# One layer of a gated linear attention trunk on one core: input rows in long runs, the first key half in the auxiliary banks, and same-place stretches of 12 products for 24

## Chip, cores and metric

One core of a Trainium2 chip (trn2). The metric is the device time of one execution in microseconds; lower is better. An execution of the kernel before takes 1075.46 us (median of three).

## What is computed

One layer on 256 tokens of width 2048: a gated linear attention mixer, then an MLP with a squared ReLU, then a final RMS norm. All weights and inputs are float32. Cut to what matters:

```python
h = rmsnorm(x, gla_norm)
proj = h @ w_in                      # q 1024, k 1024, v 2048, r 2048, g_low 16 columns
log_a = log_sigmoid(g_low @ w_gate_up + b_gate) / 16
# in chunks of 64 tokens, 4 heads:
k_dec = k * exp(total - cum)         # cum: running sum of log_a, total: its last value
state = exp(total) * state + k_dec.T @ v
o = q @ state
x = x + (rmsnorm(o, o_norm) * silu(r)) @ w_out
a = relu(rmsnorm(x, mlp_norm) @ w_up)          # 8192 columns
x = x + (a * a) @ w_down
return rmsnorm(x, final_norm)
```

## The kernel before

**Split products.** Every float32 operand of a large product is split into two parts, `hi` (rounded by ScalarE, line 109) and `lo` (the remainder, by VectorE, line 110). A product of two numbers becomes three on TensorE: `hi*hi`, `hi*lo`, `lo*hi`. Nearly all of TensorE's 9285 instructions are such products of a 128x128 stationary operand with 256 columns of a moving operand. "A product" below is one of them.

**Phases.** The work is a chain of phases on TensorE. In a *natural* phase (`natural`, products recorded on L140) tokens are stationary and a weight tile of 128 rows and 1024 columns moves: 16 steps, one for each 128 rows of the weights, and per step 2 token tiles x 3 products x 4 column quarters = 24 products. In a *turned* phase (`turned`, L169) the weights are stationary and the 256 tokens move: 8 weight tiles of two blocks of 128 rows and 512 columns, 24 products for each tile, 12 for each block. The order of phases:

1. first natural phase (half of the values and the gate's low-rank columns, 1040 columns wide), from the start to 53 us
2. turned: two halves of the keys (53 to 97 us), two halves of the queries (to 142 us)
3. natural: columns 3 x KEYW (other half of the values, to 193 us), 4 x KEYW and 5 x KEYW (the two halves of r, for the silu), then the two halves of `w_out`
4. the MLP in four rounds of 2048 hidden columns: four turned phases `up` (q 0 to 3), then `down` in two halves.

**Side work.** Small jobs (the gate's transposes and logits, `scores`, `attend`, the transposes of `turn`, the norm's `scale2_row`) wait in the queue `side`; `pump` issues one after each step (natural) or block (turned) of the main work. What is recorded is then put in order, engine by engine, by a scheduler with its own estimate of times; TensorE, ScalarE, VectorE and the DMA queue of SyncE each run their list in order.

**Where operands lie.** `OFF` is 48. Token tiles of the natural phases start 48 floats behind a multiple of 64 (`xth`, `xtl`: offset `OFF`, rows of `ROW` = 320 floats), and moving weight tiles start on a multiple of 64. In turned phases stationary weight tiles are written at `OFF` and moving tokens start on a multiple of 64. So the offset of the stationary operand, modulo 64 floats, is 48 and that of the moving one 0. Some steps break this: there both operands lie on the same offset. They are called *same-place* here:

```python
def row_x(kt):
    return [xe[:, i] for i in range(2)] if kt == EVEN else [a[:, kt, :T] for a in (xth, xtl)]
...
wh, wl = weights(w[...], 2 * GT, off=0 if kp in even else OFF)
```

`xe` holds a copy of token tile `EVEN` = 5 on a multiple of 64, for both token tiles of its step; in `turned` the argument `even` names weight tiles that are written without the offset. For `w_out` the same is done by `row_o`. In the 3 x KEYW phase step `EVEN` is put at place 11 (`late.insert(11, EVEN)`), elsewhere it stands at place 5. Each of these steps or tiles is a stretch of 24 same-place products.

**Banks.** Six PSUM banks (`acc_banks`) are given out in turn to the phases, two (`aux_bank`) to warm-up and side jobs. The first natural phase uses all six; its results leave by `put_v` (L306 on ScalarE, L307 on VectorE), and the first key half then takes the first two of the six. `turn_gate` (L334) and `gate_logits` (L343) use auxiliary banks.

**Start.** TensorE runs `WARM` products of a tile of ones (L195, two rows of the trace each). The input, transposed on the host, lies as 2048 rows of 256 floats, so a tile of 128 rows takes runs of 1 KB; tiles are loaded in groups (`x_loads`), tile 1 on ScalarE's DMA queue, the others on SyncE's between the weight tiles. The first weight tile comes in three pieces.

Of the kernel before, what the change touches and what calls it, by code (L numbers as in the profile page):

```python
# [27 lines left out]
F32 = mybir.dt.float32  # L28
F32R = mybir.dt.float32r
# [3 lines left out]
P = 128  # L33
T = 256
# [26 lines left out]
ROUNDS = HID // D  # L61
WARM = 9
FINE = 3
# [3 lines left out]
def tile_gla_mlp(ctx, tc, x, xt, cols, w_vg, w_in, w_gate, w_out, w_up, w_down, final_norm, out):  # L67
# [33 lines left out]

    def slots(off=0):
        return [wpool.tile([P, SLOT], F32R, tag=i, name=i)[:, off:] for i in ("hi", "lo")]

# [13 lines left out]

    def weights(src, n, pieces=None, room=None, skip=0, raw=None, off=0):

        to = room or slots(off)
        if raw is None:
            if not raw_half:
                raw_half.extend(raw_pair())
            raw = raw_half.pop(0)
        for s in (slice(*p) for p in pieces or [(0, n)]):
            dst = raw[:, s]
            if len(src.shape) == 3:
                dst = dst.rearrange("p (i c) -> p i c", i=2)
                last_load[0] = nc.sync.dma_start(out=dst, in_=src)  # L130
            else:
                last_load[0] = nc.sync.dma_start(out=dst, in_=src[:, s])  # L132
        return parts(raw, n, to, pieces or [(skip, n)])

    def halves(o, x, w, first, last):

        n = w.shape[-1]
        for c in range(0, n, T) if n % T == 0 else (0,):
            m = slice(c, c + T) if n % T == 0 else slice(0, n)
            nc.tensor.matmul(o[:, m], x, w[:, m], start=first and c == 0, stop=last, skip_group_check=True)  # L140

    def natural(row, source, n, cuts, pumps=1, ahead=None, order=range(KT)):

        acc = acc_banks(NT * len(cuts))
        acc = [acc[t * len(cuts) : (t + 1) * len(cuts)] for t in range(NT)]
        for step, kt in enumerate(order):
            wh, wl = weights(source(kt), n, ahead and ahead(kt))
            for t in range(NT):
                sh, sl = (a[:, t * P : (t + 1) * P] for a in row(kt))
                for i, (s, w) in enumerate(((sh, wh), (sh, wl), (sl, wh))):  # L150
                    for c, (lo, hi) in enumerate(cuts):
                        halves(acc[t][c], s, w[:, lo:hi], step == 0 and i == 0, step == KT - 1 and i == 2)
            if step < KT - 1:
                pump(pumps)
        return acc

    def turned(ah, al, w, c0, even=(0,)):

        acc = acc_banks(GT // P // 2)
        for kp in range(KT // 2):  # L160
            wh, wl = weights(w[2 * kp * P : 2 * (kp + 1) * P, c0 : c0 + GT].rearrange("(i p) c -> p i c", p=P), 2 * GT, off=0 if kp in even else OFF)
            for i in range(2):
                kt = 2 * kp + i
                for j in range(GT // P):
                    s = slice(i * GT + j * P, i * GT + (j + 1) * P)
                    o = acc[j // 2][:, j % 2 * T : (j % 2 + 1) * T]
                    for n, (u, m) in enumerate(((wh, ah), (wh, al), (wl, ah))):

                        nc.tensor.matmul(  # L169
                            o, u[:, s], m[:, kt], start=kt == 0 and n == 0 and j % 2 == 0,  # L170
                            stop=kt == KT - 1 and n == 2, skip_group_check=True,
                        )
                if kt < KT - 1:
                    pump()
        return acc
# [36 lines left out]

    xe = mid.tile([P, 2, T], F32R, tag="xe", name="xe")

    def row_x(kt):
        return [xe[:, i] for i in range(2)] if kt == EVEN else [a[:, kt, :T] for a in (xth, xtl)]

# [10 lines left out]

    xv = xt.rearrange("(kt p) t -> p kt t", p=P)
    xr = zz.rearrange("p a b t -> p (a b) t")  # L230
    cuts = [(0, 512), (512, 768), (768, WMAX)]
    x_done = [0]
    x_loads = {0: 1, 2: 4, 4: 6, 5: 8, 6: 12, 8: KT}
    nc.scalar.dma_start(out=xr[:, 1, :], in_=xv[:, 1, :])

    def input_tile(kt):
        if kt in x_loads:
            s = slice(x_done[0] if kt > 2 else kt, x_loads[kt])
            nc.sync.dma_start(out=xr[:, s, :], in_=xv[:, s, :])
            x_done[0] = x_loads[kt]  # L240
        if kt == KT - 1:
            wrap_input(0, KT - 2)
        nc.scalar.activation(xth[:, kt, :T], xr[:, kt, :], AF.Copy, scale=g1(kt))
        nc.vector.scalar_tensor_tensor(
            xtl[:, kt, :T], xr[:, kt, :], g1(kt), xth[:, kt, :T].bitcast(F32), op0=ALU.mult, op1=ALU.subtract
        )
        if kt == EVEN:
            nc.scalar.copy(xe[:, 0], xth[:, kt, :T].bitcast(F32))
            nc.vector.tensor_copy(xe[:, 1], xtl[:, kt, :T].bitcast(F32))
        return [(0, 256), (256, 512), (512, WMAX)] if kt == 0 else [(0, 512), (512, WMAX)] if kt < FINE else None  # L250

# [215 lines left out]

    late = [kt for kt in range(KT) if kt != EVEN]
    late.insert(11, EVEN)
    acc = natural(row_x, rows(w_in, 3 * KEYW), G, HALF, order=late)  # L470
    flush()
# [38 lines left out]
    def turn(src, row, gain, q):  # L510
# [5 lines left out]
        for i in range(2):  # L516
            kt = 2 * q + i
            s = b[:, i * T : (i + 1) * T]
# [12 lines left out]

    gain_o = lambda kt: go(kt % 4)
    side.extend([lambda: None] + [lambda q=q: turn(on, row_o, gain_o, q) for q in range(4)])
    acc = natural(row_x, rows(w_in, 5 * KEYW), G, HALF)
    flush()
    gate_out(acc, G)


    side.extend([lambda q=q: turn(on, row_o, gain_o, q) for q in range(4, 8)])
    hs = const.tile([P, NT, 4], F32, name="hs")  # L540

# [16 lines left out]
    hth, htl = (big.tile([P, KT, T], F32R, tag="A" + i, name="h" + i, bufs=1) for i in "hl")  # L558
    row_h = lambda kt: [a[:, kt, :] for a in (hth, htl)]
    side.extend([lambda: None] + [lambda q=q: turn(h, row_h, g2, q) for q in range(4)])  # L560
    side.append(lambda: ssq_h(0))
    acc = natural(row_o, rows(w_out, G), G, HALF)
    flush()
    add_h(acc, G)
    side.extend([lambda q=q: turn(h, row_h, g2, q) for q in range(4, 8)])
    r2 = const.tile([P, NT], F32, name="r2")
# [236 lines left out]
```

## Time and profile before

| | |
|---|---|
| time, median of 3 | 1075.46 us (1075.1 to 1075.59) |
| profiled execution, its own time | 1075.4 us |
| its span, first to last instruction | 1073.3 us |
| mean granted TensorE clock | 0.998 |
| TensorE busy | 1063.1 us, 99% |
| VectorE busy | 774.9 us, 72% |
| ScalarE busy | 573.7 us, 53% |
| data moved by DMA | 210.43 MB, mean 196 GB/s |

A line of a group reads: source line, engine, operation, output <- inputs, shape, count, then busy time and mean duration, then the idle time of the engine before it and what ended it. A line of the timeline reads: start, duration up to the last end, engine and operation, count. Products of TensorE overlap: each is under way for some 0.28 us while the next starts after some 0.11 to 0.12 us, so their durations do not add up; distances between starts do. A line of the windows gives the stretch, its length, the mean of PE, and busy time with a count for PE, PEld, DVE, ACT and POOL, then the granted clock, the DMA share and GB/s.

### The profile page before, as it was taken

How to read it: one execution, taken by the hardware profiler on the slowest of the kernel's cores; microseconds unless marked ns; L12 is line 12 of the kernel's file. 1: busy time of each engine (PE TensorE's matmuls, PEld its weight loads, DVE VectorE, ACT ScalarE, POOL GpSimd, SP SyncE). 2: the span in 40 equal slices, each digit the busy share in tenths (PEclk: the TensorE clock that was granted, in tenths of full speed). 3: DMA queues.
4: the chain of work that ended last, by engine and by line, in shares of the span. 5: the costliest groups of instructions: out<-in, count | busy, mean ns of one | idle time of the engine just before them, and what ended most of it. 6: DMA issues, size and time to landing. Idle time of an engine off the chain costs nothing.

```text
span 1073.3 us, 21863 instructions
## 1 busy us (share of the span) xinstructions
PE 1063.1 (99%) x9285; PEld 1062.3 (99%) x9285; DVE 774.9 (72%) x1027; ACT 573.7 (53%) x694; POOL 12.7 (1%) x39
## 2 busy tenths in 40 slices
PE   9999999999999999999999999999999999999997
PEld 9999999999999999999999999999999999999997
DVE  6668644556555466789986679986779997678874
ACT  6675444546444454556554456564555554555552
POOL 0000000000000000000000000000000000000000
PEclk9999999999999999999999999999999999999999
DMA  9856664556545555556566555566654666655662
GB/s 328 313 174 201 196 190 144 166 153 193 196 164 191 196 163 192 196 174 217 199 212 206 188 195 183 197 212 221 197 197 167 218 205 209 192 196 188 206 230 79
DMA packets 81009, 210.43 MB, mean 196 GB/s; under 512 B 6752, under 2 KB 9824, under 8 KB 80784
## 3 DMA queue, kind: packets, MB, share of 16 engines
q1 hardware_dynamic: 79808, 206.86, 58.4%
q10 hardware_dynamic: 1104, 2.19, 0.5%
q8 instruction: 72, 1.18, 0.4%
q14 instruction: 25, 0.20, 0.1%
HBM read 206.92 MB, written 2.10 MB: 195 GB/s over the span
## 4 chain that ended last, share of the span: by engine, by line
PE 98%; issue 1%; DMA 0%; DVE 0%; ACT 0%; SPq 0%; POOLq 0%; POOL 0%; DVEq 0%; ACTq 0%
PE acc L140 43%; PE acc L169 41%; PE aux L140 12%; PE aux L515 1%; PE aux L442 1%; DMA raw<-in_w_vg 0%; PE aux L343 0%; SPq L132 0%; DVE vl L307 0%; DVE hf L762 0%; ACT sqf L715 0%; DVE h L622 0%; ACT vh L306 0%; ACT hi L109 0%; POOLq L799 0%
## 5 line engine op out<-in xcount | busy, mean ns | idle before, releaser
L110 DVE TENSOR_TENSOR lo<-raw,hi 128x1024 fp32r<-128x1024 f32 (+3 forms) x386 | 454.3, 1178 | 242.4 <-ACT hi L109 241.2
L109 ACT CAST hi<-raw 128x1024 fp32r<-128x1024 f32 (+3 forms) x386 | 391.2, 1015 | 404.9 <-PE acc L169 175.4
L169 PE MATMUL acc<-hh,hi 128*128 128x256 f32 x1024 | 283.3, 277 | 0.0
L169 PE MATMUL acc<-hh,lo 128*128 128x256 f32 x1024 | 283.2, 277 | 0.0
L169 PE MATMUL acc<-hl,hi 128*128 128x256 f32 x1024 | 283.1, 276 | 0.0
L140 PE MATMUL acc<-hi,act 128*128 128x256 f32 x1202 | 217.3, 276 | 0.0
L169 PEld LDWEIGHTS acc<-hh,lo 128*128 128x128 f32 x1024 | 192.4, 188 | 0.0
L169 PEld LDWEIGHTS acc<-hh,hi 128*128 128x128 f32 x1024 | 192.4, 188 | 0.0
L169 PEld LDWEIGHTS acc<-hl,hi 128*128 128x128 f32 x1024 | 192.4, 188 | 0.0
L140 PEld LDWEIGHTS acc<-hi,act 128*128 128x128 f32 x1202 | 180.3, 188 | 0.0
L140 PE MATMUL acc<-lo,act 128*128 128x256 f32 x601 | 142.1, 276 | 0.0
L140 PE MATMUL aux<-hi,act 128*128 128x256 f32 x716 | 135.1, 276 | 0.0
L140 PEld LDWEIGHTS aux<-hi,act 128*128 128x128 f32 x716 | 107.9, 188 | 0.0
L140 PEld LDWEIGHTS acc<-lo,act 128*128 128x128 f32 x601 | 101.9, 188 | 0.0
L140 PE MATMUL acc<-lo,xh 128*128 128x256 f32 x480 | 77.5, 279 | 0.0
L140 PE MATMUL aux<-lo,act 128*128 128x256 f32 x358 | 76.9, 276 | 0.0
L140 PE MATMUL acc<-hi,xh 128*128 128x256 f32 x480 | 75.8, 280 | 1.0 <-ACT hi L109 1.0
L140 PE MATMUL acc<-hi,xl 128*128 128x256 f32 x480 | 76.6, 279 | 0.0
L169 PE MATMUL acc<-xh,hi 128*128 128x256 f32 x256 | 70.9, 277 | 0.4 <-DVE vl L307 0.4
L169 PE MATMUL acc<-xl,hi 128*128 128x256 f32 x256 | 71.0, 277 | 0.0
L169 PE MATMUL acc<-xh,lo 128*128 128x256 f32 x256 | 70.8, 277 | 0.0
L109 ACT CAST hi<-work 128x1024 fp32r<-128x1024 f32 x49 | 51.7, 1056 | 31.4 <-PE aux L140 12.0
(137 smaller groups left out, 1249.9 us busy)
## 6 DMA issues: line engine op xcount, KB each, us to landing
raw<-in_w_up SPq DMA_DIRECT2D x128, 512.0 KB, 4.5
raw<-in_w_down SPq DMA_DIRECT2D x128, 512.0 KB, 4.3
raw<-in_w_in SPq DMA_DIRECT2D x80, 512.0 KB, 4.7
raw<-in_w_out SPq DMA_DIRECT2D x32, 512.0 KB, 4.3
raw<-in_w_vg SPq DMA_DIRECT2D x13, 520.0 KB, 8.4
h<-in_x SPq DMA_DIRECT2D x4, 512.0 KB, 7.3
zz<-in_xt SPq DMA_DIRECT2D x2, 512.0 KB, 9.9
fb<-in_final_norm ACTq DMA_DIRECT2D x1, 1024.0 KB, 6.7
```

The source lines that it names most:

```text
L109: last_hi[0] = nc.scalar.copy(hi[:, s], raw[:, s])
L110: last_lo[0] = nc.vector.tensor_tensor(lo[:, s], raw[:, s], hi[:, s].bitcast(F32), op=ALU.subtract)
L140: nc.tensor.matmul(o[:, m], x, w[:, m], start=first and c == 0, stop=last, skip_group_check=True)
L169: nc.tensor.matmul(o, u[:, s], m[:, kt], start=kt == 0 and n == 0 and j % 2 == 0, stop=kt == KT - 1 and n == 2, skip_group_check=True,)
L442: nc.tensor.matmul(o, kab[:, k[0], c0 + c, k[1] : k[1] + P], q(qt[:, c0 + c]), start=c == 0, stop=c == 1)
L515: nc.tensor.transpose(b[:, i * T + t * P : i * T + (t + 1) * P], src[:, t, kt * P : (kt + 1) * P], ident)
```

## The change

- Same-place steps of the natural phases cover only the first token tile: 12 products. In turned phases only the second of a tile's two blocks lies in the same place: 12 products. `weights` writes such a tile in two runs with a gap of 16 floats.
- The 4 x KEYW phase takes step `EVEN` first (place 0) instead of at place 5.
- The first key half accumulates in the two auxiliary banks; `turn_gate` and `gate_logits` take banks of the six.
- The transposed input lies in DRAM as 128 rows of 16 tiles x 256 floats, so that a group of tiles is one run per row (1 KB for one tile, 2 to 4 KB and more for groups). All groups go on SyncE's queue, cut in other places. The first weight tile comes in two pieces, and `WARM` is 8.

```diff
-WARM = 9
+WARM = 8
...
-    def weights(src, n, pieces=None, room=None, skip=0, raw=None, off=0):
+    def weights(src, n, pieces=None, room=None, skip=0, raw=None, gap=None):
...
+                between = SLOT - OFF - 2 * GT if gap else 0
+                to = [a[:, OFF - between : OFF + 2 * GT + between].rearrange("p (i c) -> p i c", i=2)[:, :, between:] for a in to]
+                last_hi[0] = nc.scalar.copy(to[0], dst)
+                last_lo[0] = nc.vector.tensor_tensor(to[1], dst, to[0].bitcast(F32), op=ALU.subtract)
+                return to
...
+    def even_at(step):
+        order = [kt for kt in range(KT) if kt != EVEN]
+        order.insert(step, EVEN)
+        return order
...
-    def turned(ah, al, w, c0, even=(0,)):
-        acc = acc_banks(GT // P // 2)
+    def turned(ah, al, w, c0, even=(0,), acc=None):
+        acc = acc or acc_banks(GT // P // 2)
...
-    def row_x(kt):
-        return [xe[:, i] for i in range(2)] if kt == EVEN else [a[:, kt, :T] for a in (xth, xtl)]
+    def row_x(kt, t):
+        if kt == EVEN and t == 0:
+            return [xe[:, i] for i in range(2)]
+        return [a[:, kt, t * P : (t + 1) * P] for a in (xth, xtl)]
...
-    xv = xt.rearrange("(kt p) t -> p kt t", p=P)
+    xv = xt.rearrange("p (kt t) -> p kt t", t=T)
...
-    x_loads = {0: 1, 2: 4, 4: 6, 5: 8, 6: 12, 8: KT}
-    nc.scalar.dma_start(out=xr[:, 1, :], in_=xv[:, 1, :])
+    x_loads = {0: 1, 1: 3, 3: 6, 5: 9, 7: 12, 9: KT}
...
-        return [(0, 256), (256, 512), (512, WMAX)] if kt == 0 else [(0, 512), (512, WMAX)] if kt < FINE else None
+        return [(0, 512), (512, WMAX)] if kt < FINE else None
...
     def turn_gate():
-        b = aux_bank()
+        b = acc_banks(1)[0]
...
     def gate_logits(i):
-        b = aux_bank()
+        b = acc_banks(1)[0]
...
-        acc = turned(*xts, w_in, KEYW + half * GT, even=(0,) if half else (2,))
+        acc = turned(*xts, w_in, KEYW + half * GT, even=(0,) if half else (2,), acc=None if half else [aux_bank(), aux_bank()])
...
-    acc = natural(row_x, rows(w_in, 3 * KEYW), G, HALF, order=late)
+    acc = natural(row_x, rows(w_in, 3 * KEYW), G, HALF, order=even_at(11))
...
-    acc = natural(row_x, rows(w_in, 4 * KEYW), G, HALF)
+    acc = natural(row_x, rows(w_in, 4 * KEYW), G, HALF, order=even_at(0))
...
-    def row_o(kt):
-        c = kt * T + (OFF if kt < EVEN else 64 if kt == EVEN else OFF + 64)
-        return [a[:, c : c + T] for a in (oth, otl)]
+    def row_o(kt, t):
+        c = kt * T + t * P + (OFF if kt < EVEN else OFF + 64 if (kt, t) > (EVEN, 0) else 64)
+        return [a[:, c : c + P] for a in (oth, otl)]
...
-        "xt": x.T,
+        "xt": x.T.reshape(KT, P, T).transpose(1, 0, 2).reshape(P, KT * T),
```

`turn` writes the two token tiles of `w_out`'s input in two runs (`turned_o`), since they no longer stand side by side at `EVEN`.

More of the change, by code (lines that the diff above doesn't have):

```diff
@@ L100, in tile_gla_mlp, with slots @@
     last_load, last_hi, last_lo = [None], [None], [None]
-    def slots(off=0):
-        return [wpool.tile([P, SLOT], F32R, tag=i, name=i)[:, off:] for i in ("hi", "lo")]
+    def slots():
+        return [wpool.tile([P, SLOT], F32R, tag=i, name=i) for i in ("hi", "lo")]
     def parts(raw, n, to, pieces=None):
@@ L117, in raw_pair @@
         return a[:, :WMAX], a[:, WMAX:]
-    def weights(src, n, pieces=None, room=None, skip=0, raw=None, off=0):
-        to = room or slots(off)
+    def weights(src, n, pieces=None, room=None, skip=0, raw=None, gap=None):
+        to = room or slots()
         if raw is None:
@@ L148, in natural @@
             for t in range(NT):
-                sh, sl = (a[:, t * P : (t + 1) * P] for a in row(kt))
+                sh, sl = row(kt, t)
                 for i, (s, w) in enumerate(((sh, wh), (sh, wl), (sl, wh))):
@@ L155, in natural @@
         return acc
-    def turned(ah, al, w, c0, even=(0,)):
-        acc = acc_banks(GT // P // 2)
+    def turned(ah, al, w, c0, even=(0,), acc=None):
+        acc = acc or acc_banks(GT // P // 2)
         for kp in range(KT // 2):
-            wh, wl = weights(w[2 * kp * P : 2 * (kp + 1) * P, c0 : c0 + GT].rearrange("(i p) c -> p i c", p=P), 2 * GT, off=0 if kp in even else OFF)
+            wh, wl = weights(w[2 * kp * P : 2 * (kp + 1) * P, c0 : c0 + GT].rearrange("(i p) c -> p i c", p=P), 2 * GT, gap=kp in even)
             for i in range(2):
@@ L536, in tile_gla_mlp @@
     gate_out(acc, G)
-    side.extend([lambda q=q: turn(on, row_o, gain_o, q) for q in range(4, 8)])
+    side.extend([lambda q=q: turn(on, turned_o, gain_o, q) for q in range(4, 8)])
     hs = const.tile([P, NT, 4], F32, name="hs")
@@ L564, in tile_gla_mlp @@
     add_h(acc, G)
-    side.extend([lambda q=q: turn(h, row_h, g2, q) for q in range(4, 8)])
+    side.extend([lambda q=q: turn(h, turned_h, g2, q) for q in range(4, 8)])
     r2 = const.tile([P, NT], F32, name="r2")
```

28 lines of the change are left out of this document (16 added, 12 removed).

## The prediction

> **What bounds the kernel now.** I read the page first.
>
> ```profile
> span 1073.3 us, 21863 instructions
> PE 1063.1 (99%) x9285; PEld 1062.3 (99%) x9285; DVE 774.9 (72%) x1027; ACT 573.7 (53%) x694; POOL 12.7 (1%) x39
> ...
> PEclk9999999999999999999999999999999999999999
> ...
> PE 98%; issue 1%; DMA 0%; DVE 0%; ACT 0%; SPq 0%; POOLq 0%; POOL 0%; DVEq 0%; ACTq 0%
> ```
>
> TensorE is busy for 99% of the span at a clock that is not held back, and 98% of the chain that ended last is its own. So the time is the number of its products (one matmul each) times the distance from one start to the next, plus the few places where it waits. The number hardly changes. Busy time cannot show the distance, because products overlap; a window's length over its count can. Next, therefore, the windows (length, then PE busy and count):
>
> ```profile
> 79.50:142.00 62.50, 62.50 (x553) 62.50 (x553) 46.21 (x79) 32.57 (x39) 2.33 (x16) 1.00 0.65 200
> 181.60:211.10 29.50, 29.50 (x253) 29.50 (x252) 16.20 (x19) 15.00 (x20) 1.64 (x3) 1.00 0.60 179
> 214.10:250.70 36.60, 36.60 (x325) 36.60 (x325) 20.30 (x24) 19.00 (x25) 2.19 (x4) 1.00 0.57 170
> 263.70:293.50 29.80, 29.80 (x265) 29.80 (x264) 15.42 (x15) 14.37 (x16) 0.00 (x0) 1.00 0.59 195
> ```
>
> A product is under way for 0.28 us, so a window counts about 2.5 that began before it. 62.50 / 550.5 is 113.5 ns and 36.60 / 322.5 is 113.5 ns, but 29.50 / 250.5 is 117.8 ns, with the same 128x256 shapes and no wait. TensorE has two paces, and it stays in one of them. Before and after each window stands a stretch of 24 same-place products (both operands on the same offset modulo 64 floats; elsewhere they are 48 apart). The timeline gives where stretches begin, and one where an even pace came before:
>
> ```profile
> 178.74 0.65 PE L140 MATMUL acc<-hi,xe 128*128 128x256 f32 x4
> 211.30 0.64 PE L140 MATMUL acc<-hi,xe 128*128 128x256 f32 x4
> 260.87 0.60 PE L140 MATMUL acc<-hi,xe 128*128 128x256 f32 x3
> 306.49 0.64 PE L140 MATMUL acc<-hi,oth 128*128 128x256 f32 x4
> 309.37 0.50 PE L140 MATMUL acc<-hi,oth 128*128 128x256 f32 x3
> 398.42 0.36 PE L169 MATMUL acc<-hh,lo 128*128 128x256 f32 x1
> ```
>
> From 306.49 to 309.37 there are 24 products: 120.0 ns each, the dearest pace of the three. But the tile views (shortest/median/longest duration, first start) say what the stretch does:
>
> ```profile
> L140 PE MATMUL acc<-hi,xe x10: 280/284/287, 179.8 to 181.4; 128*128 128x256 f32 x10
> L140 PE MATMUL acc<-hi,xe x11: 283/283/283, 212.2 to 213.9; 128*128 128x256 f32 x11
> L140 PE MATMUL acc<-hi,xe x8: 283/283/283, 262.1 to 263.5; 128*128 128x256 f32 x8
> L169 PE MATMUL acc<-hh,hi x5: 283/283/283, 399.7 to 401.1; 128*128 128x256 f32 x5
> L169 PE MATMUL acc<-xh,hi x6: 283/283/283, 60.0 to 61.8; 128*128 128x256 f32 x6
> ```
>
> In four stretches the durations become one single value, 283 ns, from 212.2, 262.1, 399.7 and 60.0 on; the stretches that began at 211.30, 260.87 and 398.42 had run 0.9, 1.2 and 1.3 us, some 8, 10 and 11 products. Behind them follows 113.5 ns (the windows from 214.10 and 263.70). The one of 178.74 never came to a single value, and behind it follows 117.8 ns for 29.7 us, until the next stretch. So a same-place stretch is a reset: it costs 120.0 instead of 113.5, and when it settles, the 113.5 pace holds until odd-shaped products (transposes, scores) break it. The change halves these stretches.
>
> **Stretches halved.** Thirteen stretches (one in each of the six natural phases that have `EVEN`, two in the key halves, two in the first MLP round, one in each later) give up 12 products. Nine of them (second key half, value gate 4, 5, both `w_out` halves, `up` from round 0, q 1 on) give these to the 113.5 pace: 9 x 12 x 6.5 ns = 0.70 us. Four lie beside the 117.8 pace (first phase, first key half, 3 x KEYW, first `up`): 4 x 12 x 2.2 = 0.11 us. Both hold only if 12 settle as 24 did. From an even pace that is sure. Behind odd shapes the rows say 8 to 11 products. The order of the built program leaves 11 of the 12 behind the transposes of the 5 x KEYW phase, where 10 were needed: just enough. In the first `up` twelve shifted products now stand between the diagonal products and the stretch, so its entry is one the trace does not show.
>
> **One stretch at step 0.** The stretch of 178.74 is entered as before and should fail as before. Then before ran 29.7 us / 117.8 ns = 252 products slowly. Now 12 (second token tile of step 11) and 4 x 24 run slowly, then the 4 x KEYW phase opens with its stretch. Apart from the 12 counted above, 252 - 96 = 156 products go from 117.8 to 113.5: 156 x 4.3 ns = 0.67 us. It enters from a long 117.8 pace, as that of 211.30 did, which settled in 8. No queue is passed but SP's: weight tile 5 is loaded first instead of sixth, same size.
>
> At this place a rule of the Trainium skill speaks against the change: "TensorE: Matmul & The Clock Gate", section "Step-by-step: what each phase is for", says that TensorE has two independent read ports into SBUF, so that loading the next weights takes nothing from the product that streams. By it, place has no price and no effect, and the terms of these two parts (0.70 + 0.11 + 0.67) would be zero. The rows above, 120.0 against 113.5 ns for one shape, disagree; I go by the rows.
>
> **First key half in the auxiliary banks.** Behind the first phase TensorE waits for an accumulator (chain in order of time, then timeline):
>
> ```profile
> 52.47 0.76 DVE vl L307
> ...
> 53.27 2.74 PE acc L169 x21
> 52.21 0.64 PE L140 MATMUL acc<-hi,xl 128*128 128x256 f32 x4
> 53.50 0.28 PE L169 MATMUL acc<-xl,hi 128*128 128x256 f32 x1
> 55.26 1.14 ACT L320 ACTIVATE gn<-acc,r 128x16 f32<-128x16 f32 x6
> 54.33 1.08 ACT L109 CAST hi<-raw 128x1024 fp32r<-128x1024 f32 x1
> ```
>
> Four products from 52.21 would end their turns at 52.68; the next starts at 53.27, held by `put_v`, and the second 0.23 us later instead of 0.12. That is 0.59 + 0.11 = 0.70 us. The two auxiliary banks have been idle since warm-up, so nothing takes the wait's place. The gate's five banks come from the other pool. Its first transpose needs the `gn` copies, done at 56.4 now and, with one more `hi` split (1.08) put between them by the built order, at 57.5; it stands 47 products behind the start of the half, at 52.68 + 47 x 0.118 = 58.2. If the cover went, the transpose would wait in line with all TensorE work; at most the 0.70 comes back.
>
> **Start: long runs, two pieces for three, eight warm products.**
>
> ```profile
> 1.16 0.42 SPq L132
> ...
> 2.10 4.41 DMA raw<-in_w_vg
> ...
> 6.53 0.64 ACT hi L109
> ...
> 7.21 2.91 PE acc L140 x22
> 1.04 4.15 PE L195 MATMUL aux<-ones 128*128 128x128 f32 x18 [1.04 <-DVE ones L192]
> 4.91 0.56 PE L140 MATMUL acc<-hi,xh 128*128 128x256 f32 x2
> raw<-in_w_vg SPq DMA_DIRECT2D x3, 264.0 KB, 5.1
> raw<-in_w_vg SPq DMA_DIRECT2D x2, 128.0 KB, 2.8
> ```
>
> Six products run from 4.91, then TensorE waits until 7.21 for the third piece of the first weight tile. Now the first piece is 256 KB, issued at 1.16: at the 128 KB rows' 2.8 us it lands at 3.9, at the 264 KB row's 5.1 us at 6.3. The 128 KB of input tile 1 no longer travel ahead on ScalarE's queue, so I take 4.1; with the 0.64 of the larger `hi` row the first products start at 4.8, behind eight warm products (each of the nine, two rows of 4.91 - 1.04 = 3.87 us over 18, takes 0.43, so they end at 4.5). The second piece is issued (2.10 - 1.16) / 2 = 0.47 earlier than the third was, with one 128 KB transfer fewer ahead. I take a landing near 5.6 for 6.51; `hi` 0.64; TensorE goes on at 6.3, 0.9 us earlier, but with 2 products done instead of 6, which is 4 x 0.118 = 0.5 back, and 0.1 for starting sooner: 0.5 us gained. Bounds: no wait left at all would give 7.21 - 4.91 - 6 x 0.118 = 1.6 us; the first piece landing at 6.3 (TensorE at 6.9, all 24 products still to do against 18 at 7.21) loses 0.4. Later input loads in runs of 2 to 4 KB end no wait that the chain shows.
>
> The rest (`xe` of one token tile, gaps in `turned_o` and in two-run splits) rides on ACT at 53% and DVE at 72%; I put it at nothing, and a few 0.05 us if a split were late.
>
> **Sum** against the profiled execution, 1075.4 us (span 1073.3 and 2.1 around it; the median 1075.46 is 0.06 above): 0.70 + 0.11 + 0.67 + 0.70 + 0.5 = 2.7 us, so 1072.7 us, 0.25% less. About 0.2%, 2.15 us, is what a measurement of this kernel can tell from no change.
>
> **Rivals.**
> - *The stretch at step 0 does not settle*, as that of 178.74 did not. For: one of five entries off an even pace failed. Against: the nearest like entry, 211.30, settled. Then the 372 other products of the phase, 72 of the attention and 48 of the next phase, 492 in all, stay slow: 492 x 4.3 = 2.1 us, leaving 1074.8. Same. Chance 0.15.
> - *Twelve are too few in the MLP.* The first `up` stretch has an untried entry; if it fails, the next one (q 1, a few products on) starts from the 117.8 pace instead of an even one, and if it fails too, nothing resets until round 1: 60 + 553 + 726 + 11 = 1350 products (the rest of q 0 behind the first stretch, of q 1 to 3, `down`, and the start of round 1, by the built order) x 4.3 = 5.8 us: 1078.5. Slower. It decides at whether one of these two settles within 12. For: needs of 8 to 11 leave little room. Against: four of five settled. Chance 0.13.
> - *The start gives nothing or loses*: bound -0.4 to 0, the rest as forecast: 1073.2 to 1073.6. Same. Chance 0.15.
> - *Place plays no part*; the paces are set by what else happens at these points, so halving and moving does nothing: only 0.70 + 0.5 are left, 1074.2. Same. It is what the skill's rule above would make of it; the tile rows speak against it. Chance 0.04.
>
> **How the numbers follow.** The forecast has the remaining 0.53; its own range goes from 1071.5 (start at 1.6) to 1073.2. The range for 8 in 10 reaches over the start, the place and the step-0 rivals to 1075.3 (the step-0 stretch lost with a start of 0), and leaves out the MLP rival: 1071.5 to 1075.3. Faster 0.52 (the forecast less its rim), same 0.35 (three rivals and the rim), slower 0.13.
>
> **What would show it.** Right: a window behind the step-0 stretch at 113.5 ns up to the first transposes; tile rows with one single duration in the last of the 12 products; no gap before the first L180 product; the first wait ending near 6.3. Wrong: durations of 280 to 287 at a stretch's end and 117.8 behind it, above all in `up` of round 0; or a first wait that ends after 7.2 with few products done.

## The result and the profile after

The changed kernel takes 1073.38 us (median of 20 runs, 1072.71 to 1075.01) against 1075.40 us (20 runs of before on the same chip): ratio 0.9981, 95% interval 0.9975 to 0.9987, so 2.0 us less, of 2.7 forecast. The profiled execution has a span of 1071.1 and a time of its own of 1072.98 us, 2.2 and 2.4 less than that of before. The page after, its first lines and the chain:

```profile
span 1071.1 us, 21851 instructions
PE 1061.8 (99%) x9283; PEld 1060.9 (99%) x9283; DVE 775.1 (72%) x1026; ACT 574.2 (54%) x693; POOL 12.7 (1%) x39
...
PE 96%; DMA 1%; issue 1%; ACT 0%; DVE 0%; SPq 0%; POOLq 0%; POOL 0%; DVEq 0%; ACTq 0%
```

TensorE still sets the time, but DMA now stands in the chain with 1%; where that is comes below. First the windows (length, then PE busy and count):

```profile
78.00:140.50 62.50, 62.50 (x554) 62.50 (x553) 44.93 (x78) 31.03 (x36) 2.35 (x16) 1.00 0.66 203
181.00:190.00 9.00, 9.00 (x79) 9.00 (x78) 3.68 (x3) 3.67 (x4) 0.00 (x0) 1.00 0.70 216
194.00:248.50 54.50, 54.50 (x483) 54.50 (x483) 30.93 (x38) 27.18 (x38) 4.40 (x8) 1.00 0.56 167
```

With the 2.5 products taken off that began before a window, 54.50 / 480.5 is 113.4 ns: the step-0 stretch has put the whole 4 x KEYW phase on the fast pace. Ahead of it, 9.00 / 76.5 is still 117.6: the stretch of the 3 x KEYW phase failed again. The timeline has the first row of both stretches, now of twelve products each, and of what follows the second:

```profile
177.43 0.65 PE L146 MATMUL acc<-hi,xe 128*128 128x256 f32 x4
191.59 0.64 PE L146 MATMUL acc<-hi,xe 128*128 128x256 f32 x4
193.02 0.62 PE L146 MATMUL acc<-hi,xh 128*128 128x256 f32 x4
```

The `xe` tile in the stretch of each phase (shortest/median/longest duration, first and last start):

```profile
L146 PE MATMUL acc<-hi,xe x8: 280/283/287, 177.4 to 178.8; 128*128 128x256 f32 x8
...
L146 PE MATMUL acc<-hi,xe x8: 278/282/283, 191.6 to 192.9; 128*128 128x256 f32 x8
```

In the second none is above 283; in the first they run up to 287.

How far after is ahead of before, at the same product in both traces (starts in us, before minus after):

```
first product of the first key half          53.27   52.19  1.08
second product of it                         53.50   52.31  1.19
last product ahead of the 3 x KEYW stretch  178.62  177.31  1.31
last product ahead of the transposes        250.78  248.67  2.11
last product of the 5 x KEYW phase          293.62  291.73  1.89
start of the last MLP round's down          980.80  978.41  2.39
last product of all                        1065.35 1062.96  2.39
end of the span                            1073.29 1071.06  2.24
```

So 1.19 come from the start and the bank (its second product too came later than its turn in before), 0.12 from the key halves, 0.80 from there to the end of the 4 x KEYW phase, 0.22 are lost again in the 5 x KEYW phase, among its transposes, 0.50 come from the shorter stretches up to the last round, and 0.15 are lost behind the last product.

The bank wait is gone. The last four products of the first phase and the first of the key half:

```profile
51.71 0.65 PE L146 MATMUL acc<-hi,xl 128*128 128x256 f32 x4
52.19 0.28 PE L180 MATMUL aux<-xh,hi 128*128 128x256 f32 x1
52.31 0.28 PE L180 MATMUL aux<-xl,hi 128*128 128x256 f32 x1
```

52.19 - 51.71 is 0.48, four pitches of 0.12, and the second product follows 0.12 later.

The start is another matter. The timeline of the first products:

```profile
4.69 0.80 PE L146 MATMUL acc<-hi,xh 128*128 128x256 f32 x2
5.77 0.54 PE L146 MATMUL acc<-hi,xh 128*128 128x256 f32 x2 [0.28 <-ACT hi L109]
6.62 0.64 PE L146 MATMUL acc<-hi,xh 128*128 128x256 f32 x4
7.09 0.40 PE L146 MATMUL acc<-lo,xh 128*128 128x256 f32 x2
```

and of the chain up to 25 us (start, length, what):

```profile
8.57 9.81 DMA zz<-in_xt
...
18.41 0.32 ACTq L284
...
18.77 2.19 ACT xh L255 x6
...
21.19 0.50 ACT xh L255
21.68 0.27 ACT xh L233
21.96 0.97 ACT hi L109
...
22.95 1.25 DVE lo L110
...
24.25 0.87 PE acc L146 x5
```

The first wait ends at 5.77, earlier than the 6.3 I had put, and at the ninth product after is 0.95 us ahead of before (6.62 for 7.56). But the last input group, tiles 12 to 15 in one transfer (rows of 4 KB, the longest here), is under way for 9.81 us and lands at 18.4. Until then ScalarE stands at the issue of a gate load (L284). Then it makes the `xh` of seven tiles in a row (9 to 15; the first three had landed at 15.9), and only afterwards the next `hi` split. In before it makes four in a row at this place. The size of the transfer and the two rows of ScalarE, after and then before:

```profile
zz<-in_xt SPq DMA_DIRECT2D x1, 512.0 KB, 9.8
18.77 2.91 ACT L255 ACTIVATE xh<-zz,colt 128x256 fp32r<-128x256 f32 x7 [2.68 <-DMA zz<-in_xt]
20.25 1.71 ACT L243 ACTIVATE xh<-zz,colt 128x256 fp32r<-128x256 f32 x4 [3.65 <-DMA raw<-in_w_vg]
```

TensorE waits twice between 22.8 and 24.3, 0.49 us in all by its pitches (a pitch is the distance from one start to the next). Of the 0.95 us gained at the front, 0.50 are left behind it (24.98 for 24.48).

### The profile page after: what moved, and what is told of

It is laid out like the page before. It is cut to its first block, busy times and chain, and to the rows that moved or that the text cites. A ratio compares the mean times of both kernels' runs of the same rounds, so it can differ in the third digit from the quotient of the medians.

```text
span 1071.1 us, 21851 instructions
## 1 busy us (share of the span) xinstructions
PE 1061.8 (99%) x9283; PEld 1060.9 (99%) x9283; DVE 775.1 (72%) x1026; ACT 574.2 (54%) x693; POOL 12.7 (1%) x39
## 4 chain that ended last, share of the span: by engine, by line
PE 96%; DMA 1%; issue 1%; ACT 0%; DVE 0%; SPq 0%; POOLq 0%; POOL 0%; DVEq 0%; ACTq 0%
PE acc L146 42%; PE acc L180 39%; PE aux L146 12%; PE aux L180 2%; DMA zz<-in_xt 1%; PE aux L525 1%; PE aux L454 1%; DMA raw<-in_w_vg 0%; ACT xh L255 0%; SPq L138 0%; DVE lo L110 0%; ACT hi L109 0%; PE acc L355 0%; SPq L251 0%; DVE hf L779 0%
## 5 line engine op out<-in xcount | busy, mean ns | idle before, releaser
L110 DVE TENSOR_TENSOR lo<-raw,hi 128x1024 fp32r<-128x1024 f32 (+2 forms) x225 | 258.5, 1151 | 123.2 <-ACT hi L109 122.2
L109 ACT CAST hi<-raw 128x1024 fp32r<-128x1024 f32 (+2 forms) x225 | 223.4, 994 | 214.9 <-PE acc L146 115.5
L135 DVE TENSOR_TENSOR lo<-raw,hi 128x1024 fp32r<-128x1024 f32 x160 | 195.7, 1224 | 115.3 <-ACT hi L134 114.6
L134 ACT CAST hi<-raw 128x1024 fp32r<-128x1024 f32 x160 | 168.1, 1051 | 187.5 <-PE acc L180 144.7
L146 PE MATMUL acc<-lo,xh 128*128 128x256 f32 x496 | 79.7, 279 | 0.1
L146 PE MATMUL acc<-hi,xh 128*128 128x256 f32 x496 | 78.7, 281 | 0.3 <-ACT hi L109 0.3
L146 PE MATMUL acc<-hi,xl 128*128 128x256 f32 x496 | 78.8, 278 | 0.0
L146 PEld LDWEIGHTS acc<-hi,xh 128*128 128x128 f32 x496 | 66.7, 188 | 0.8 <-ACT hi L109 0.7
```

The source lines that it names most:

```text
L109: last_hi[0] = nc.scalar.copy(hi[:, s], raw[:, s])
L110: last_lo[0] = nc.vector.tensor_tensor(lo[:, s], raw[:, s], hi[:, s].bitcast(F32), op=ALU.subtract)
L134: last_hi[0] = nc.scalar.copy(to[0], dst)
L135: last_lo[0] = nc.vector.tensor_tensor(to[1], dst, to[0].bitcast(F32), op=ALU.subtract)
```

## The experiments

A time below is the median of its runs in the same comparison as before. The first four ran beside a before of 1075.29, the next four beside 1075.10, three beside 1075.31 and the last beside 1075.22.

**The bank alone undone.**

```
- acc = turned(..., acc=None if half else [aux_bank(), aux_bank()])   # key half
+ acc = turned(...)
- b = acc_banks(1)[0]      # turn_gate, gate_logits
+ b = aux_bank()
```

> The changed kernel with the first key half back in the six banks and the gate's jobs back in the auxiliary ones; all else as changed. Reset theory (a same-place stretch costs 120 ns a product but puts TensorE back on the 113.5 ns pace; each part of the change adds its own term): the wait of about 0.6 us behind the first phase comes back, the stretches settle as before, time 0.7 us above the changed kernel's 1073.4, so 1074.1. Rival (the bank wait was hidden behind something else, place has no effect): no more than 0.2 us above it.

Measured 1073.65 us (1073.12 to 1074.42, 11 runs), ratio 0.9986 [0.9977, 0.9995], span 1071.6. The old wait is back, in the timeline

```profile
52.00 0.64 PE L146 MATMUL acc<-hi,xl 128*128 128x256 f32 x4
52.94 0.39 PE L180 MATMUL acc<-xh,hi 128*128 128x256 f32 x1 [0.29 <-DVE vl L319]
53.17 0.28 PE L180 MATMUL acc<-xl,hi 128*128 128x256 f32 x1
```

and in the chain:

```profile
52.14 0.76 DVE vl L319
52.90 0.04 issue
52.94 3.10 PE acc L180 x24
```

0.94 - 0.48 is 0.46, and 0.11 at the second product: 0.57 of the 0.70 us, on the path. At that product this kernel is 0.86 us behind the changed one (53.17 for 52.31); the other 0.29 come from the first phase, where its wait near 22.8 was longer in this execution. At the last product 0.57 are left in all, since 0.25 come back in the 5 x KEYW transposes (see start_back). The term stands in its place; its effect on the median, 0.27, is within the spread.

**The start alone undone.**

```
- WARM = 8
+ WARM = 9
...
- xv = xt.rearrange("p (kt t) -> p kt t", t=T)
+ xv = xt.rearrange("(kt p) t -> p kt t", p=P)
...
- x_loads = {0: 1, 1: 3, 3: 6, 5: 9, 7: 12, 9: KT}
+ x_loads = {0: 1, 2: 4, 4: 6, 5: 8, 6: 12, 8: KT}
+ nc.scalar.dma_start(out=xr[:, 1, :], in_=xv[:, 1, :])
...
- return [(0, 512), (512, WMAX)] if kt < FINE else None
+ return [(0, 256), (256, 512), (512, WMAX)] if kt == 0 else [(0, 512), (512, WMAX)] if kt < FINE else None
```

> The changed kernel with the old input layout, the old load groups, three pieces of the first weight tile and nine warm products. Reset theory: TensorE waits until 7.2 us again for the third piece, but the wait of 0.49 us in the changed kernel's first phase near 22.8 us (a group of seven input tiles landing at 18.4 us) goes too, so only 0.4 us are lost: 1073.8. The changed kernel's executions fall into two groups 1.4 us apart; if the late input group makes them, one group is left here; if a short stretch does that settles in some executions only, two are left. Rival (the whole gain is the start): 1075.4, no gain left.

Measured 1072.92 us (1072.65 to 1073.44, 11 runs), ratio 0.9979 [0.9970, 0.9987], span 1071.0: not 0.4 us slower, as was expected, but as fast as the changed kernel or faster. (The group that landed at 18.4 has four tiles, not seven as the expectation says; seven is what ScalarE made in a row.) The first wait is the old one, and none follows at 22.8:

```profile
7.14 1.00 PE L146 MATMUL acc<-hi,xh 128*128 128x256 f32 x6 [0.56 <-ACT hi L109]
```

It reaches the stretch of the second key half 0.45 us behind the changed kernel (77.14 for 76.69), but its span is no longer. Where 0.3 of this goes stands in the chain of the 5 x KEYW phase. Two pieces of it, of before:

```profile
251.49 2.73 PE acc L140 x24
254.22 0.44 PE aux L515 x4
```

of after:

```profile
249.39 2.83 PE acc L146 x24
252.22 0.44 PE aux L525 x4
```

of this kernel:

```profile
249.83 2.73 PE acc L146 x24
252.56 0.44 PE aux L526 x4
```

Between one group of four transposes and the next stand 24 products; they take 2.73 us in before and here, 2.83 in after. Three such groups make 0.3. The same instructions in the same order: the pace in which TensorE leaves the transposes differs from kernel to kernel, and no part of the change is meant to touch it. Of the kernels with same-place stretches, before, start_back, bank_back, all_24 and start_turned keep the faster pace there, and the others lose it; why, no run shows.

**All stretches at 24 again, the rest kept.** 

```
- xe = mid.tile([P, 2, P], F32R, tag="xe", name="xe")     # one token tile
+ xe = mid.tile([P, 2, T], F32R, tag="xe", name="xe")     # both
- wh, wl = weights(..., 2 * GT, gap=kp in even)
+ wh, wl = weights(..., 2 * GT, off=0 if kp in even else OFF)
... row_x and row_o alike, for both token tiles
```

> The changed kernel with stretches of 24 products everywhere; step 0, banks and start as changed. Reset theory: 12 more products at 120 ns in each of 13 stretches, 0.70 + 0.11 us, so 1074.2; if the two groups of the changed kernel's times come from a stretch that is just too short, they merge here. Rival (place plays no part in the pace): no difference, 1073.4, and two groups remain.

Measured 1073.70 us (1072.83 to 1075.02, 11 runs), ratio 0.9986 [0.9978, 0.9995], span 1071.7, 0.6 more than after. At the last product it is 0.67 us behind the changed kernel: 0.19 from the first phase, some 0.7 from the longer stretches (0.81 were worked out), and 0.22 come back in the 5 x KEYW transposes. Twelve give what 24 gave: every stretch that settled at 24 (pitches of 120 up to its end, 113.3 behind it) settles at 12 too, that of `up` in round 0 at its sixth product.

**The 4 x KEYW stretch back at step 5.**

```
- acc = natural(row_x, rows(w_in, 4 * KEYW), G, HALF, order=even_at(0))
+ acc = natural(row_x, rows(w_in, 4 * KEYW), G, HALF)
```

> The changed kernel with the 4 x KEYW phase in its old order, the same-place step at place 5 instead of 0. Reset theory: the 117.8 ns pace lasts about 156 products longer, 156 x 4.4 ns = 0.7 us, so 1074.1, with 117.8 ns from 179 to 209 us and 113.3 behind it. Rival (place plays no part): no difference, 1073.4.

Measured 1073.68 us (1073.37 to 1075.33, 11 runs), ratio 0.9989 [0.9980, 0.9998], span 1071.6. The stretch begins at 209.86 and settles; the products ahead of it run at 117.8. From the 3 x KEYW stretch to that of 5 x KEYW it takes 82.44 us (177.21 to 259.65), after 81.75 (177.31 to 259.06): 0.69, against 0.67 forecast. The starts are those of the last product ahead of the first stretch and of the first product behind the transposes in the second. The medians are 0.30 apart.

**No same-place product at all.** 

```
- if kt == EVEN and t == 0:
-     return [xe[:, i] for i in range(2)]
...
- between = SLOT - OFF - 2 * GT if gap else 0
+ between = 0
...
- c = kt * T + t * P + (OFF if kt < EVEN else OFF + 64 if (kt, t) > (EVEN, 0) else 64)
+ c = kt * T + t * P + (OFF if (kt, t) <= (EVEN, 0) else OFF + 64)
```

> The changed kernel with no same-place product anywhere: the first token tile of step EVEN is read from the same shifted tiles as the rest, and the two-run splits and the attention rows get no offset back. Same number of products, shapes and bytes. Reset theory: nothing puts TensorE back to 113.3 ns after the first break, so most of the 9,000 products go at 117.8 or, where the entry happens to be even, at 113.3: the span grows by 25 to 36 us, to 1098 to 1110. If place plays no part: within 1 us of the changed kernel, 1073.

Measured 1105.95 us (one run), span 1104.0: 33 us more. A window deep in the MLP:

```profile
560.00:900.00 340.00, 340.00 (x2889) 340.00 (x2888) 269.87 (x350) 176.59 (x186) 0.00 (x0) 1.00 0.57 192
```

340 / 2886.5 is 117.8 ns. Without the stretches the slow pace lasts to the end. This settles the rival that place plays no part. The prediction had tied that rival to the rule of the Trainium skill ("TensorE: Matmul & The Clock Gate", section "Step-by-step: what each phase is for") that loading the next weights takes no read bandwidth from the product that streams. The measurement decides against the rival; whether the read ports are where place acts, no run shows.

**The step-0 stretch cut to four products.**

```
+ def row_short(kt, t):
+     whole = [a[:, kt, t * P : (t + 1) * P] for a in (xth, xtl)]
+     return [whole[0], xe[:, 1]] if kt == EVEN and t == 0 else whole    # only the low part is same-place
...
- acc = natural(row_x, rows(w_in, 4 * KEYW), ..., order=even_at(0))
+ acc = natural(row_short, rows(w_in, 4 * KEYW), ..., order=even_at(0))
```

> The changed kernel with the step-0 stretch of the 4 x KEYW phase cut from 12 products to 4 (only the products of the low part are same-place). Reset theory: this stretch needed 7 products, so 4 do not settle it; the 492 products behind it stay at 117.8 instead of 113.3: + 2.2 us, near 1075.5. Rival (any touch of a same-place product resets, or the length plays no part): 1073.4, and 113.3 from 192.9 on.

Measured 1077.25 us (one run), span 1075.3. The window 196.0 to 248.5 of this kernel,

```profile
196.00:248.50 52.50, 52.50 (x448) 52.50 (x447) 27.45 (x35) 24.22 (x35) 4.39 (x8) 1.00 0.52 155
```

and of after:

```profile
196.00:248.50 52.50, 52.50 (x466) 52.50 (x465) 29.85 (x37) 27.12 (x38) 4.40 (x8) 1.00 0.55 163
```

52.50 / 445.5 is 117.8 against 52.50 / 463.5 = 113.3. Four do not reset (all four are products of the low part, in one run). From the last product ahead of the stretch of the first key half (61.36, in after 59.28) to the first behind the transposes in that of 5 x KEYW (263.31, 259.06) it takes 201.95 us against 199.78: 2.17, as forecast. The other 2.1 us of its span are at the start, and have another cause (banks_turned, below).

**The last input group split in two.** The edit loads tiles 12 and 13, and later 14 and 15; that the group has the tiles 9 to 15, as the expectation says, is wrong.

```
- x_loads = {0: 1, 1: 3, 3: 6, 5: 9, 7: 12, 9: KT}
+ x_loads = {0: 1, 1: 3, 3: 6, 5: 9, 7: 12, 9: 14, 11: KT}
```

> The changed kernel with its last input group (tiles 9 to 15) loaded as two, 9 and 10 and later 11 to 15. If the late landing of this group makes the wait at 22.8 us and the upper group of the runs: the wait goes, 1072.8, and the runs are one group. If the upper group comes from elsewhere: the wait goes in the profile, median near 1073, still two groups 1.4 us apart.

Measured 1073.06 us (1072.71 to 1073.36, 10 runs), ratio 0.9977 [0.9968, 0.9987], span 1070.9. The chain now goes from the first weight tile straight into TensorE, without input DMA:

```profile
5.45 0.64 ACT hi L109
6.09 0.04 issue
6.13 18.97 PE acc L146 x156
```

The wait at 22.8 is gone, 0.49 us: ScalarE now makes five `xh` tiles in a row ahead of the next `hi` split, not seven. In this execution the first wait ended 0.36 later, at 6.13. That no upper group showed in ten runs was chance, as place_12 and banks_turned tell, which have the same start.

**The 3 x KEYW stretch one step later** (with the split group).

```
- acc = natural(row_x, rows(w_in, 3 * KEYW), G, HALF, order=even_at(11))
+ acc = natural(row_x, rows(w_in, 3 * KEYW), G, HALF, order=even_at(12))
```

> As split_group, and the stretch of the 3 x KEYW phase one step later (place 12 for 11), so that it is entered from a long 117.8 pace instead of from behind the scores. Theory (the entry decides): it settles as the step-0 stretch did, 72 to 84 products at 113.3 for 117.8, - 0.3 to - 0.4 us against split_group: 1072.5. Rival (something in this phase keeps it from settling): durations of 280 to 287 to its end, and the time of split_group.

Measured 1072.97 us (1072.44 to 1075.44, 11 runs), ratio 0.9981 [0.9972, 0.9990]. Two of its runs lie in the upper group. My theory falls: entered from a steady pace of 117.8, it fails as before.

```profile
L146 PE MATMUL acc<-hi,xe x8: 280/283/287, 180.0 to 181.3; 128*128 128x256 f32 x8
```

**The accumulators of its two token tiles exchanged** (with the split group).

```
+ acc = acc[::-1]          # natural(), in the 3 x KEYW phase alone
```

> As split_group, with the two token tiles of the 3 x KEYW phase in each other's accumulator banks; the stretch is at place 11 again. Theory (the banks decide): in place_12 the same operand addresses failed that settle in the 5 x KEYW phase, from a steady 117.8 pace; what is left is that this stretch alone writes banks 0 and 1. In the banks 3 and 5 it settles: one duration, 283, at its end, and 108 products behind it (96 to the end of the phase and the first of the next) at 113.3 for 117.8, - 0.48 us: 1072.6 against 1073.06. Rival (the phase's entry or what runs beside it): the 117 121 120 124 cycle again, and 1073.0 to 1073.1.

Measured 1073.14 us (1072.55 to 1075.19, 11 runs). The edit came to nothing: in the built program banks go by first write, and the stretch still writes the same two (the traces do not name banks). For the stretch it tells nothing. It serves as a repeat of split_group, and its profiled execution was one of the long ones, span 1073.0. The timeline from the warm products on:

```profile
4.54 0.79 PE L146 MATMUL acc<-hi,xh 128*128 128x256 f32 x2
6.81 0.81 PE L146 MATMUL acc<-hi,xh 128*128 128x256 f32 x2 [1.47 <-ACT hi L109]
...
8.27 1.07 PE L146 MATMUL acc<-hi,xh 128*128 128x256 f32 x4
9.13 0.63 PE L146 MATMUL acc<-lo,xh 128*128 128x256 f32 x2
```

The window 6.8 to 10.0 of this kernel,

```profile
6.80:10.00 3.20, 3.19 (x15) 3.19 (x16) 3.18 (x6) 3.07 (x6) 0.00 (x0) 1.00 1.03 369
```

and of split_group:

```profile
6.80:10.00 3.20, 3.20 (x29) 3.20 (x28) 2.89 (x7) 2.55 (x5) 0.00 (x0) 1.00 1.05 378
```

Behind a wait that ended at 6.81, four products take 0.86 us (8.27 to 9.13), 0.215 each, where after takes 0.47 (6.62 to 7.09). Half as many products fit into 3.2 us, with TensorE busy throughout. The short_4 profile has the same: a wait from 4.9 to 6.9, then products 213 to 214 ns apart up to 10.1 (fourteen, where I had counted sixteen for the expectations below). From the end of the first wait to the stretch of the first key half it takes 54.52 us here (6.81 to 61.33) and 53.02 in split_group (6.13 to 59.15): 1.5 us lost, about the distance between the two groups of times that the changed kernel has (13 runs at 1072.71 to 1073.57, 7 at 1074.37 to 1075.01). The granted clock in these rows is 1.00, so that column doesn't show it.

When the half pace began, the durations tell (shortest/median/longest): those of the last warm products and of the two products ahead of the wait, in this kernel

```profile
L207 PE MATMUL aux<-ones x5: 420/421/422, 3.6 to 4.4; 128*128 128x128 f32 x5
L146 PE MATMUL acc<-hi,xh x2: 415/498/581, 4.5 to 4.9; 128*128 128x256 f32 x2
```

and in split_group:

```profile
L206 PE MATMUL aux<-ones x5: 275/317/421, 3.6 to 4.2; 128*128 128x128 f32 x5
L146 PE MATMUL acc<-hi,xh x2: 279/334/388, 4.6 to 4.8; 128*128 128x256 f32 x2
```

So the wait did not slow TensorE down. In every trace it starts slow: the rows of the warm products are 421 ns long and 213 ns apart. In split_group it came to the full pace within the warm products, whose last rows are 275 ns long and 111 apart. In the twelve other traces the first short duration stands between 4.0 and 7.4 us. In this one and in short_4 TensorE was still slow when it ran out of work at about 5.3 for some 1.5 us, and came to the full pace only at 10.2. (In after and in start_back it was still slow at a shorter wait, of 0.28 and 0.56 us, and came to the full pace right behind it.) The Trainium skill does know such a state: "TensorE: Matmul & The Clock Gate", section "What's actually happening", has a clock of 1.2 GHz by default, which some 3.4 us of sustained work release to 2.4, by a window that runs free of the kernel. An estimate from it, 256 columns at 1.2 GHz, is 213 ns, and the trace agrees with that, and nearly with the length (3.2 us from 6.81).

**The same exchange on start_back.**

> As start_back (old input layout, load groups, pieces and nine warm products), with the banks of the 3 x KEYW phase exchanged. If the banks decide: 1072.92 - 0.48 = 1072.4. If not: 1072.9. In both the runs form one group and no wait stands at 22.8 us.

Measured 1072.92 us (1072.44 to 1073.31, 9 runs), ratio 0.9973 [0.9963, 0.9983]; the stretch unchanged for the same reason. A repeat of start_back, again one group.

**Old load groups on the new layout.** Long runs, two pieces and eight warm products are kept.

```
- x_loads = {0: 1, 1: 3, 3: 6, 5: 9, 7: 12, 9: KT}
+ x_loads = {0: 1, 2: 4, 4: 6, 5: 8, 6: 12, 8: KT}
+ nc.scalar.dma_start(out=xr[:, 1, :], in_=xv[:, 1, :])
```

> The changed kernel with its long DRAM runs, two pieces and eight warm products kept, but the old input load groups (tile 1 by itself on ScalarE's queue, then 2-3, 4-5, 6-7, 8-11, 12-15). If the grouping alone makes the wait at 22.8 us and the upper group of times: both are gone; the first wait ends near 6.0 to 6.5 since 128 KB travel ahead again, 1073.0. If the long runs or the pieces make the upper group: it stays.

Measured 1073.02 us (1072.54 to 1075.02, 11 runs), ratio 0.9980 [0.9971, 0.9989]; three runs above 1074.2. The wait at 22.8 is gone and the upper group stays: it does not come from the input groups. The last group here has four tiles as well (512 KB), but ScalarE makes only four `xh` in a row: the wait goes with the seven in a row, not with the size of the transfer. In this profile the first products start at 5.89 and the first wait ends at 6.62.

**Ten warm products, and the second token tile first in the 3 x KEYW phase** (with the split group).

```
- WARM = 8
+ WARM = 10
- for t in range(NT):
+ for t in tiles:          # (1, 0) in the 3 x KEYW phase
```

> As split_group, with ten warm products for eight, and in the 3 x KEYW phase the second token tile before the first, which puts the stretch in the banks 3 and 5 (0 and 1 so far) and twelve shifted products ahead of it. Start: the warm products end near 5.4 instead of 4.5, so a second piece that lands late (6.8) ends a wait of about 1.2 us instead of 1.9, and the sixteen products at 213 ns that followed the waits of 1.9 us do not come: one group of times, nothing above 1073.9. If the upper group has another cause: it stays. Stretch: if the banks decide, it settles and 96 products go at 113.3 for 117.8, - 0.42: 1072.6; if its phase decides, the 117 121 120 124 cycle again and 1073.0.

Measured 1073.09 us (1072.32 to 1073.51, 11 runs), ratio 0.9979 [0.9970, 0.9988]. One group: of the eight kernels with eight warm products and more than one run, 23 of 96 runs lie above 1074.1; of the three with nine or ten (start_back, start_turned, this one) none of 31. That is a hint and no proof. Of the three kernels that have this start but eight warm products (split_group, place_12, banks_turned) 6 of 32 lie there, and at that rate none in eleven comes about one time in ten. And before has nine warm products too, yet 11 of its 113 runs lie 1.0 to 2.9 us above their median, of which no trace was kept. The profiled execution has the shortest span of all, 1070.3: TensorE came to the full pace within the warm products, at 4.8, and there is no first wait.

```profile
5.03 1.00 PE L146 MATMUL acc<-hi,xh 128*128 128x256 f32 x4
```

The stretch, now in other banks (by the built program those in which the 5 x KEYW stretch settles) and from a steady 117.8 pace, failed once more, with the same cycle of pitches. So it is not the banks either.

No kernel that was run beats the changed one beyond its interval. Those with the lowest medians, 1072.9 to 1073.1, are the ones in which the upper group or the wait at 22.8 is missing.

## Why the prediction was right, and where it was off

The forecast was 1072.7, the range 1071.5 to 1075.3; measured 1073.38. By the prediction's own bound the result, -0.19% with an interval from -0.25 to -0.13, lies on the rim between faster and the same. The 0.7 us that are missing have their places: in the profiled executions 2.39 of the 2.7 are there at the last product, 0.22 to 0.3 having gone among the transposes; 0.15 are lost behind the last product; and the median lies 0.4 above the profiled execution, which is one of the shorter ones, while a third of the runs are some 1.4 us longer.

- *Stretches halved, 0.81.* Right. All that settled at 24 settle at 12. In the MLP, 0.50 from the w_out phases to the last round against 0.49 by the prediction's terms for the seven stretches there; the key halves gave 0.12 for 0.11. `xe` of 5 x KEYW had eleven products behind the transposes and settled at the tenth, as forecast just enough. The entry in `up` that the trace had not shown settled at the sixth, so the rival on 1078.5 did not come.
- *Stretch at step 0, 0.67.* Right: up to the transposes 0.80 were gained, 0.10 of them from the halving by the prediction's terms; undoing it cost 0.69. It settled at its seventh product. The rival that it does not settle is what short_4 makes by force, 2.17 us for the 2.1 worked out.
- *The 3 x KEYW stretch fails.* Right as a forecast, but the reason it gave was the entry ("entered as before"), and that is wrong: place_12 and warm_10 enter from a steady 117.8 pace and fail too.
- *Bank, 0.70.* Right: no wait stands there now, and the lead grows from 0.50 to 1.19 over it. The cover of the gate's transposes held.
- *Start, 0.5.* Here the number is luck. In the profiled execution 0.50 are left, but of two errors that cancel. The first half was too low: the wait ended at 5.77, not 6.3, and 0.95 were gained. And the prediction put the later input loads at nothing, because they ended no wait in the chain of before; cut anew, they make ScalarE take seven tiles in a row, which costs TensorE 0.49. What it also did not consider is that TensorE starts at half pace, though its own row of the warm products has it (two rows in 0.43 us, where they take 0.22 at the full pace): if the second piece is late before TensorE has come to the full one, fourteen products run at half pace behind the wait, 1.5 us. A third of the changed kernel's runs lie higher by about this. That this lengthens them is shown in two profiled executions of other kernels with the same first loads; of the changed kernel itself no such execution was profiled. By the medians the start is worth nothing (start_back 1072.92): undone, it costs 0.44 in the first phase of the profiled execution, and 0.3 of this comes back in the transposes. That is the rival "the start gives nothing", 1073.2 to 1073.6, and 1073.38 lies in it; its mechanism was the landing of the first piece, and is not what happened.
- *No term for the transposes.* 0.22 to 0.3 were lost among the 5 x KEYW transposes. The prediction said that only a window up to the first transposes would be fast, and put no price on the pace that the transposes leave behind; start_back and bank_back show that it can come out either way.
- *The rival that place plays no part.* Ruled out by none_same, 33 us.

What stays open is why the 3 x KEYW stretch never settles; it fails in every trace that has it, with 24 products (before, all_24) as with 12. The starts in the trace say only what goes with it. The slow pace is a beat of nine products (117 118 118 118 117 118 118 117 119, mean 117.8). Pitches in ns from the last product ahead of the stretch on (its start stands first), and how many products before it the beat's last 119 stood:

```
after      191.48   4 before   115 117 118 119 121 117 117 120 120   settles
place_12   191.24   1 before   115 116 119 119 121 116 118 120 120   settles
bank_back  192.34   7 before   115 117 118 120 120 117 118 120 120   settles
place_12   179.91   8 before   117 121 120 124 118 117 121 120 124   does not
warm_10    177.99   8 before   117 121 120 124 118 117 121 120 124   does not
```

Steps have 24 products and token tiles 12, multiples of three, so moving the stretch by a step or a tile cannot take it from 8 to 1, 4 or 7. That would fit, and one odd product ahead of the stretch would try it; it was not tried, and what the beat is was not shown.

## What to carry to other kernels

Where busy time stands at 99%, divide a window by its count: a pace that is 4% slower shows there, and busy time hides it. When input loads are grouped anew, ask what the engine that takes them will do in a row, and what queues behind it; that the old groups ended no wait says nothing of the new ones. And judge a start by many runs, and see at which pace the warm products end: the gain of an early first product can be paid back by a wait that comes while TensorE is still at half pace. More warm products may guard against that; the runs here do not settle it.

## What was not expected of the hardware

- TensorE starts at half pace in all fourteen traces (rows of the warm products 213 ns apart), and comes to the full one between 4.0 and 7.4 us in twelve of them. In the two in which it was still slow and then idle for some 1.5 us, 128x256 products took 213 ns each for the 3.2 us behind that. The granted clock is shown as 1.00 throughout.
- In the changed kernel a same-place stretch that starts from the slow pace comes to steady pitches of 120 ns at its sixth to tenth product, and 113.3 follows for 117.8; four products do not bring it, and in the 3 x KEYW phase 24 do not. Without any stretch, 117.8 holds for hundreds of microseconds.
- Four input tiles in one transfer (512 KB) were under way for 9.81 us beside the weight loads.
